# Last half of a DiT block: w_down and the second MLP product accumulated token by token in PSUM

## The chip, the cores and the metric

The kernel runs on one core of one Trainium2 chip. The core has TensorE (PE in the profile: matmuls, with the loads of the stationary operand as PEld), VectorE (DVE), ScalarE (ACT), GpSimd (POOL) and SyncE (SP, which issues nearly all DMAs). Matmuls write into PSUM, eight banks of 128 partitions x 512 fp32; DVE and ACT read the sums from there. The metric is the device time of one launch in microseconds (us), lower is better; for a kernel the median of several runs is given.

## The reference

A diffusion backbone of two layers on 256 latent tokens and 256 context tokens, 1024 features, all in fp32. Layer 0 mixes tokens with a convolution module, layer 1 with a bidirectional mLSTM of 4 heads of 512. After each mixer and each MLP stands a LayerNorm. In the last layer only the latent tokens are needed behind the mixer. The part that the change is about is the end of layer 1:

```python
def sq_relu_mlp(u, w1, w2):
    return jnp.square(jax.nn.relu(u @ w1)) @ w2
...
    y = (hn.astype(xc.dtype) + skip * xc) * jax.nn.silu(z)
    return y @ w_down                                  # (256 x 2048) @ (2048 x 1024)
...
        h = layer_norm(ALPHA * h + g1 * y, ln1_g[i], ln1_b[i])
        h = layer_norm(ALPHA * h + g2 * sq_relu_mlp(modulate(h, sh2, sc2), mlp_w1[i], mlp_w2[i]), ln2_g[i], ln2_b[i])
```

w1 is 1024 x 4096, w2 is 4096 x 1024. g1, g2, sh2 and sc2 are vectors over the 1024 features, made from the condition.

## The kernel before

**Products.** Each fp32 operand is split in two fp32r parts, hi and lo, and a product is hi·hi + hi·lo + lo·hi: three matmuls into one PSUM bank. `mm3` (L176 to L181) keeps a 128x128 block of the weight stationary and streams activations, so its result has features on the partitions and tokens along the row. `mm3t` (L183 to L187) keeps the activations of 128 tokens stationary and streams 512 columns of the weight, so its result has tokens on the partitions. Matmuls of the latent tokens alone stream 256 columns under `mm3`, and 512 under `mm3t`.

**Weights.** `raw_load` (L148) has SP fetch 1 MB at a time into one of three staging buffers `raw`. `split_w` cuts it in two pieces of 128x1024; ACT casts each to `wh` (L154), DVE subtracts to get `wl` (L155). There are four `wh` and four `wl` buffers (NW), handed out in turn; a staging buffer is free again after the lo split of its second piece. Other tiles come from pools in the same way: a piece of code that gets a buffer waits for the last reader of what it held.

**Order.** The code is written in the order of the computation, with some steps mixed by hand; a scheduler then fixes the order on each engine and puts in the semaphores. On each engine instructions run strictly in that order, so an instruction that waits holds up all behind it.

**The end of layer 1.** `Z.att` (L46) is the list of main and side steps of the attention part, run by the loop at L1378: `oN` is the o gate of head N, `G` `W` `A` are decay, weights and attend, `DN` is w_down of head N. A side step is advanced a number of times for each step of the main one. D0 runs beside o2, D1 and D2 beside A3, D3 by itself.

`down(h)` (L1354) takes the head's 512 rows of w_down and makes, for each of 8 blocks m of 128 features, 4 x 3 matmuls of 256 columns. A DVE instruction (L1366) then adds gate times the sum to the residual `hl[m]`, which lies feature by feature; this happens for each head. For the last head `hl[m]` also goes to `Norm.feed` (L417), which builds sums for the LayerNorm on DVE and ACT.

`ln.finish` (L446) sums over the partitions with small PE matmuls (L441), takes the root on ACT (L455), builds a diagonal (L462) and spreads the result over the rows with a matmul by ones (L467). `ln.apply` (L473, L474) normalises each block, and L1405 to L1407 make the MLP's input `u2`, hi on ACT and lo on DVE.

`mlp` (L823) runs in four chunks of 1024 hidden features: w1 for 8 blocks m (three matmuls of 256 columns for each of 8 kt), squared ReLU and split, then w2 for 8 blocks of output features, whose sums DVE adds to the residual (L854) after each chunk. A second Norm, the affine part on ACT (L1421) and eight transfers of 128 KB (L1422) of a features x tokens result end the kernel; the host transposes it. Creating a Norm puts a small Sqrt activation (`warm`, L403) into ACT's stream, which the scheduler has at the program's start.

## Time and profile before

| | us |
|---|---|
| median of 3 runs | 1737.08 (1736.88 to 1744.12) |
| the profiled execution | 1738.46 |
| its span in the profile | 1736.7 |
| PE busy | 1691.6 (97%) |
| DVE busy | 1071.7 (62%) |
| ACT busy | 736.3 (42%) |

The span is the stretch that the profile shows, from the first to the last recorded work; the rest of the time lies around it. In a timeline each row has the start, the duration, engine, line of the kernel, operation, output and input by name, and in brackets how long the engine stood idle before it and what ended that. Matmuls are pipelined: their durations overlap, and what one costs is read from the distance of the starts. "mm", "ln", "fl" and "cv" are names of PSUM banks (3, 2, 1 and 2 of them), the others are tiles in SBUF.

### The profile page before, as it was taken

The numbers are of one execution on the slowest core, as the hardware profiler recorded it, in microseconds if no ns is written. First come the engines' busy times: TensorE is split into PE (matmuls) and PEld (weight loads), VectorE is DVE, ScalarE is ACT, GpSimd is POOL, SyncE is SP. The second block draws the span as 40 slices with busy tenths as digits, with TensorE's granted clock in tenths as the row PEclk, the third lists the DMA queues.
The fourth block names the chain that finished last, engine by engine and source line by source line (L and its number), as shares of the span: only waits on it lengthen the run. The fifth ranks groups of instructions, "written<-read, shape, count | busy, mean of one in ns | idle before, by whom it ended". The sixth has DMA issues, their size and how long they took to land.

```text
span 1736.7 us, 25617 instructions
## 1 busy us (share of the span) xinstructions
PE 1691.6 (97%) x10282; PEld 1443.4 (83%) x10282; DVE 1071.7 (62%) x1975; ACT 736.3 (42%) x1159; POOL 31.8 (2%) x84
## 2 busy tenths in 40 slices
PE   8999999999999999999999999999999999989996
PEld 5655798888888999976787999998777888979996
DVE  5556897976665886762222543443687766886666
ACT  3411763232324465542333433432576645444443
POOL 0000000000000000000000000000021000000000
PEclk9999999999999999999999999999999999989998
DMA  9333534665554065577743622443545555535551
GB/s 359 128 118 122 215 126 146 218 218 194 194 194 170 28 220 170 160 237 253 264 146 126 223 99 96 150 157 132 183 158 188 186 206 204 184 112 180 189 176 49
DMA packets 60182, 298.61 MB, mean 172 GB/s; under 512 B 5986, under 2 KB 21858, under 8 KB 26656
## 3 DMA queue, kind: packets, MB, share of 16 engines
q1 hardware_dynamic: 42400, 282.29, 46.6%
q10 hardware_dynamic: 17664, 14.69, 2.5%
q8 instruction: 81, 1.33, 0.3%
q14 instruction: 37, 0.30, 0.1%
HBM read 281.22 MB, written 15.73 MB: 171 GB/s over the span
## 4 chain that ended last, share of the span: by engine, by line
PE 92%; DVE 3%; ACT 2%; DMA 1%; issue 1%; POOL 0%; SPq 0%; POOLq 0%; ACTq 0%
PE mm L177 23%; PE mm L181 23%; PE mm L180 23%; PE mm L187 3%; PE mm L185 3%; PE mm L186 3%; PE fl L297 1%; PE fl L647 1%; PE cv L716 1%; DVE wl L155 1%; PE ln L177 1%; PE ln L180 1%; PE ln L181 1%; DMA raw<-ada_w 1%; PE cv L185 1%
## 5 line engine op out<-in xcount | busy, mean ns | idle before, releaser
L155 DVE TENSOR_TENSOR wl<-raw,wh 128x1024 fp32r<-128x1024 f32 x354 | 432.4, 1225 | 357.7 <-ACT wh L154 356.9
L154 ACT CAST wh<-raw 128x1024 fp32r<-128x1024 f32 x354 | 368.2, 1048 | 615.0 <-PE mm L180 432.8
L180 PE MATMUL mm<-u,wh 128*128 128x256 f32 (+1 forms) x1400 | 447.2, 320 | 0.0
L177 PE MATMUL mm<-u,wh 128*128 128x256 f32 (+1 forms) x1272 | 397.7, 314 | 6.6 <-DVE E L673 2.0
L181 PE MATMUL mm<-u,wl 128*128 128x256 f32 (+1 forms) x1272 | 396.8, 313 | 1.1 <-DVE wl L155 1.1
L180 PEld LDWEIGHTS mm<-u,wh 128*128 128x128 f32 x1400 | 268.2, 192 | 18.4 <-DVE mv L482 0.8
L177 PEld LDWEIGHTS mm<-u,wh 128*128 128x128 f32 x1272 | 243.2, 192 | 30.5 <-issue 5.6
L181 PEld LDWEIGHTS mm<-u,wl 128*128 128x128 f32 x1272 | 244.3, 192 | 16.3 <-DVE wl L155 2.3
L177 PE MATMUL mm<-hid,wh 128*128 128x256 f32 (+1 forms) x512 | 165.9, 324 | 0.0
L180 PE MATMUL mm<-hid,wh 128*128 128x256 f32 (+1 forms) x512 | 165.3, 323 | 0.0
L181 PE MATMUL mm<-hid,wl 128*128 128x256 f32 (+1 forms) x512 | 165.3, 323 | 0.0
L177 PEld LDWEIGHTS mm<-hid,wh 128*128 128x128 f32 x512 | 97.4, 190 | 7.9 <-issue 0.2
L180 PEld LDWEIGHTS mm<-hid,wh 128*128 128x128 f32 x512 | 97.4, 190 | 7.7 <-issue 0.2
L181 PEld LDWEIGHTS mm<-hid,wl 128*128 128x128 f32 x512 | 97.4, 190 | 7.6
L177 PE MATMUL mm<-xm,wh 128*128 128x512 f32 x256 | 102.9, 402 | 0.0
L185 PE MATMUL mm<-wh,xl 128*128 128x512 f32 x256 | 101.0, 396 | 0.7 <-ACT wh L154 0.6
L186 PE MATMUL mm<-wh,xl 128*128 128x512 f32 x256 | 100.6, 393 | 0.6 <-DVE xl L155 0.6
L181 PE MATMUL mm<-xm,wl 128*128 128x512 f32 x256 | 100.3, 392 | 0.0
L187 PE MATMUL mm<-wl,xl 128*128 128x512 f32 x256 | 100.1, 394 | 0.2
L177 PE MATMUL mm<-qq,wh 128*128 128x272 f32 x256 | 73.9, 289 | 0.0
L180 PE MATMUL mm<-qq,wh 128*128 128x272 f32 x256 | 73.9, 289 | 0.0
L181 PE MATMUL mm<-qq,wl 128*128 128x272 f32 x256 | 73.8, 288 | 0.0
(411 smaller groups left out, 2745.7 us busy)
## 6 DMA issues: line engine op xcount, KB each, us to landing
raw<-w SPq DMA_DIRECT2D x64, 1024.0 KB, 4.9
raw<-ada_w SPq DMA_DIRECT2D x48, 1024.0 KB, 5.3
raw<-wo SPq DMA_DIRECT2D x32, 1024.0 KB, 4.9
raw<-wv SPq DMA_DIRECT2D x16, 1024.0 KB, 6.5
raw<-wqT SPq DMA_DIRECT2D x16, 1024.0 KB, 5.1
raw<-wq SPq DMA_DIRECT2D x16, 1024.0 KB, 4.9
raw<-wk SPq DMA_DIRECT2D x16, 1024.0 KB, 4.9
raw<-pw SPq DMA_DIRECT2D x10, 1024.0 KB, 6.2
```

The costliest lines, as they stand in the source:

```text
L154: c = nc.scalar.copy(hi, src)
L155: nc.vector.tensor_tensor(lo, src, hi.bitcast(F32), op=ALU.subtract)
L177: a = nc.tensor.matmul(ps, wh, xh, start=start, stop=False)
L180: nc.tensor.matmul(ps, wh, xl, start=False, stop=False)
L181: nc.tensor.matmul(ps, wl, xh, start=False, stop=stop)
L185: nc.tensor.matmul(ps, xh, wh, start=start, stop=False)
L186: nc.tensor.matmul(ps, xl, wh, start=False, stop=False)
L187: nc.tensor.matmul(ps, xh, wl, start=False, stop=stop)
L297: a = nc.tensor.matmul(ps[32 * j:32 * j + 32], cs[:, kt, 14 - 2 * v:46 - 2 * v], blocks[kt], start=first and kt < 4, stop=last and kt >= 4 ...
L647: nc.tensor.matmul(wqs[0][32 * j:32 * j + 32, :], wgp[0][:, kt, :], raw[:, j * 512:(j + 1) * 512], start=kt == 0, stop=kt == ET - 1, tile_ ...
L716: return nc.tensor.matmul(o[r:r + 64, :], g_[:, r:r + 64], ps_[b][i], start=i == 0, stop=i == 1, tile_position=(0, r))
```

## The change

Four things change, all in layer 1.

1. **Token-major residual.** `hl` becomes four tiles `hl[t][h_]`: 128 tokens (t) by 512 features (h_). In up_z a new side step `rows()` fills them: 8 DVE instructions, 16 PE transposes and 4 copies on ACT.
2. **w_down.** `down(h)` uses `mm3t`: activations stationary, weights streamed 512 wide, the sum of all heads in four PSUM banks `dacc` (three "mm" and the "fl"), 192 matmuls of 512 in place of 384 of 256. The host lays `wdown` out anew. D0 leaves the side of o2 and stands with D1 and D2, beside A3. The last head has its weights split in pieces of 512 and its matmuls grouped by (t, h_); after each group DVE multiplies by the gate's row, adds to `hl` and takes bn_stats. The gate's rows come from a small DRAM tile (written by ACT's queue during layer 0) broadcast to 128 partitions. The LayerNorm becomes a row-wise one: aggregate, Sqrt, reciprocal and a subtract-and-multiply on DVE, then 16 transposes back to features, from which `affine_half` makes `u2`, with hi and lo side by side in one tile of 512 columns.
3. **MLP.** For a block of w1 one matmul streams hi and lo together (512 columns, stationary `wh`) and one streams hi alone (256 columns, stationary `wl`); ACT copies the lo half of the sum, DVE adds it and squares. The w2 product is an `mm3t` with the hidden activations stationary, summed over all 32 blocks in four banks (two "ln", two "cv"). Two blocks of w1 and two of w2 alternate. The last four w2 blocks are grouped by (t, h_).
4. **Tail.** Five rows of 1024 (gain and bias of both LayerNorms, the gate) are broadcast to 128 partitions; DVE finishes the LayerNorm row-wise, and four transfers of 256 KB write the output token by token.

```diff
-    att = [['o0', 'G0 W0 W1', 2], ['o1', 'A0 W2', 1.6], ['o2', 'A1 W3 D0', 2.1], ['o3', 'A2', 1], ['D1 D2', 'A3', 1.2], ['D3', '', 0]]
+    att = [['o0', 'G0 W0 W1', 2], ['o1', 'A0 W2', 1.6], ['o2', 'A1 W3', 1.6], ['o3', 'A2', 1], ['D0 D1 D2', 'A3', 1.2]]
...
+    g_dr = [dp.tile([D], F32, name=f"g_dr{i}") for i in range(2)]
+    for i, o in enumerate((2 * DT, 5 * DT)):
+        nc.scalar.dma_start(g_dr[i].rearrange("(f p) -> p f", p=P), ada[1][:, o:o + DT, 1])
...
-                for kt in range(4):
-                    mm3(ps, *kcol(w, (i % 2) * 4 + kt), *yy[h][kt], kt == 0, kt == 3)
-                nc.vector.scalar_tensor_tensor(hl[m], ps, g1[:, m:m + 1], hl[m], op0=ALU.mult, op1=ALU.add)
...
+        if last:
+            for t in range(2):
+                for h_ in range(2):
+                    for kt in range(4):
+                        down_mm(h, kt, t, h_, ws[kt])
+                    tm, r = tmp("E"), hl[t][h_]
+                    nc.vector.tensor_tensor(tm, dacc[t, h_], g1r[h_], op=ALU.mult)
+                    nc.vector.tensor_tensor(r, r, tm, op=ALU.add)
+                    nc.vector.bn_stats(st1[:, t, h_, :], r)
+                    yield
+
+    def down_mm(h, kt, t, h_, w):
+        yh, yl = yy[h][kt]
+        mm3t(dacc[t, h_], yh[:, BLK[t]], yl[:, BLK[t]], w[0][h_], w[1][h_], h == 0 and kt == 0, h == H - 1 and kt == 3)
...
+        root(mv1[:, t], st1[:, t])
+        for h_ in range(2):
+            nc.vector.tensor_scalar(hl[t][h_], hl[t][h_], mv1[:, t, 0:1], mv1[:, t, 2:3], op0=ALU.subtract, op1=ALU.mult)
+            for j in range(4):
+                f = 4 * h_ + j
+                nc.tensor.transpose(trs[f // 2][:, f % 2 * C + t * P:f % 2 * C + (t + 1) * P],
+                                    hl[t][h_][:, j * P:(j + 1) * P], ident)
...
+        affine_half(t[:, LO], t[:, HI], trs[f // 2][:, f % 2 * C:f % 2 * C + C], 1, ca, cb, f)
...
+    for r, src in zip(rws, [rows_d[i] for i in range(4)] + [g_dr[1]]):
+        nc.sync.dma_start(r, row(src))
...
+        a = lambda stop: nc.tensor.matmul(ps, wh, u2[kt], start=kt == 0, stop=stop)
+        b = lambda: nc.tensor.matmul(ps[:, LO], wl, u2[kt][:, LO], start=False, stop=False)
...
+        mm3t(facc[t, h_], hid[j][:, t * P:(t + 1) * P], hid[j][:, C + t * P:C + (t + 1) * P], w[0][:, sl], w[1][:, sl],
+             j == 0, j == NF - 1)
...
+    for m in range(4, NF, 2):
+        up(m)
+        up(m + 1)
+        dn(m - 4)
+        dn(m - 3)
+        if m == 6:
+            for t in range(2):
+                for h_ in range(2):
+                    r, sl = hl[t][h_], slice(h_ * T, (h_ + 1) * T)
+                    nc.vector.scalar_tensor_tensor(r, r, ALPHA, ln1g[:, sl], op0=ALU.mult, op1=ALU.mult)
+                    nc.vector.scalar_tensor_tensor(r, ln1b[:, sl], ALPHA, r, op0=ALU.mult, op1=ALU.add)
...
+            nc.vector.tensor_tensor(tm, facc[t, h_], g2r[:, sl], op=ALU.mult)
+            nc.vector.tensor_tensor(r, r, tm, op=ALU.add)
+            nc.vector.bn_stats(st1[:, t, h_, :], r)
+        root(mv1[:, t], st1[:, t])
...
-    ln.finish()
-    for f in range(DT):
-        xn = ln.apply(f)
-        t = tmp("E")[:, :C]
-        nc.scalar.activation(t, xn, AF.Identity, scale=V("ln2_g1", f), bias=V("ln2_b1", f))
-        nc.sync.dma_start(out[f * P:(f + 1) * P, :], t)
```

The scheduler's order shows where steps now stand. The line numbers in rows of the changed kernel are its own.

First SP's queue at the end of w_down, before. `raw` is a staging buffer, `wdown` w_down, `zs_dr` the stored z gate of a head, and `w_1` stands for both weights of the second MLP:

```order
L150 DMA raw_13164<-v_dr_5290 128x2048
L150 DMA raw_13250<-wdown 128x2048
L150 DMA raw_13330<-zs_dr_5294 128x2048
L150 DMA raw_13351<-wdown 128x2048
L150 DMA raw_13441<-wdown 128x2048
L150 DMA raw_13507<-wdown 128x2048
L150 DMA raw_13578<-wdown 128x2048
L150 DMA raw_13686<-w_1 128x2048
L150 DMA raw_13696<-w_1 128x2048
```

And in the changed kernel, up to the broadcasts of the five rows:

```order
L150 DMA raw_13321<-wdown 128x2048
L150 DMA raw_13355<-w_1 128x2048
L150 DMA raw_13365<-w_1 128x2048
L150 DMA raw_13375<-wdown 128x2048
L150 DMA raw_13393<-wdown 128x2048
L150 DMA raw_13664<-w_1 128x2048
L150 DMA raw_13722<-w_1 128x2048
L150 DMA raw_13756<-w_1 128x2048
L1464 DMA row_13554<-rows_d 128x1024
L1464 DMA row_13555<-rows_d 128x1024
L1464 DMA row_13558<-g_dr_5302 128x1024
L150 DMA raw_13814<-w_1 128x2048
```

The first two loads of w1 now stand ahead of the last head's two loads of w_down, and the five rows stand between loads of the MLP's weights.

Second, DVE behind the LayerNorm of w_down's result, before (`lc` are the small statistics, `S` and `u` make the lo part of the MLP's input):

```order
L458 SCALAR_TENSOR_TENSOR lc_13721<-lc_13709,lc_13721 128x2
L462 TENSOR_TENSOR L_13724<-ident,lc_13721 128x512
L473 TENSOR_TENSOR hl_5901<-hl_5901,ln_13726 128x256
L474 TENSOR_TENSOR hl_5901<-hl_5901,ln_13726 128x256
L473 TENSOR_TENSOR hl_5901<-hl_5901,ln_13726 128x256
L1406 TENSOR_SCALAR S_13743<-hl_5901,ca_13729,cb_13730 128x256
```

And in the changed kernel (`mv` are mean and deviation, `row` the broadcast rows; L497 writes the lo part):

```order
L1411 BN_AGGR mv_11256<-st_11255 128x2
L1413 RECIPROCAL mv_11256<-mv_11256 128x1
L1445 TENSOR_SCALAR hl_5307<-hl_5307,mv_11256 128x512
L1445 TENSOR_SCALAR hl_5308<-hl_5308,mv_11256 128x512
L1537 SCALAR_TENSOR_TENSOR hl_5305<-hl_5305,row_13554 128x512
L1537 SCALAR_TENSOR_TENSOR hl_5306<-hl_5306,row_13554 128x512
L497 TENSOR_TENSOR u_13514<-S_13515,u_13514 128x256
L497 TENSOR_TENSOR u_13519<-S_13520,u_13519 128x256
L1538 SCALAR_TENSOR_TENSOR hl_5305<-row_13555,hl_5305 128x512
L497 TENSOR_TENSOR u_13524<-S_13525,u_13524 128x256
```

The scaling of the residual by the gain's row (L1537), which the code writes inside the MLP's loop, stands ahead of the lo parts of the MLP's input.

Third, PE in the MLP of the changed kernel, the end of one block of w1 and the start of a block of w2 (`hid` are the hidden activations):

```order
L1470 MATMUL mm_14810<-u_13544,wh_14806 128x512
L1471 MATMUL mm_14810<-u_13544,wl_14807 128x256
L1471 MATMUL mm_14810<-u_13549,wl_14807 128x256
L1470 MATMUL mm_14810<-u_13549,wh_14806 128x512
L185 MATMUL ln_13660<-wh_14836,hid_14619 128x512
L186 MATMUL ln_13660<-wh_14836,hid_14619 128x512
L187 MATMUL ln_13660<-wl_14837,hid_14619 128x512
L185 MATMUL ln_13661<-wh_14836,hid_14619 128x512
```

Before, all rows of the MLP are of the form of this one, in threes by L177, L180 and L181:

```order
L177 MATMUL mm_14480<-u_13756,wh_14518 128x256
L180 MATMUL mm_14480<-u_13756,wh_14518 128x256
L181 MATMUL mm_14480<-u_13756,wl_14519 128x256
L177 MATMUL mm_14480<-u_13763,wh_14518 128x256
L180 MATMUL mm_14480<-u_13763,wh_14518 128x256
```

Two matmuls of 512 and 256 columns take the place of three of 256 in the first product; in the second the sums stay in the four banks from one block to the next.

More of the change, by code (lines that the diff above doesn't have):

```diff
@@ L1371, in chain, with row, root @@
+    def row(src):
+        return src.rearrange("(o c) -> o c", o=1).broadcast_to([P, src.shape[0]])
+    def root(mv, st):
+        nc.vector.bn_aggr(mv[:, 0:2], st.rearrange("p h c -> p (h c)"))
+        nc.scalar.activation(mv[:, 2:3], mv[:, 1:2], AF.Sqrt, bias=eps)
+        nc.vector.reciprocal(mv[:, 2:3], mv[:, 2:3])
+    g1r = []
     def chain(names):
         for n_ in names.split():
-            if n_[0] == "D":
-                yield from down(int(n_[1]), "mm" if main_is_down else "fl")
-            else:
-                yield from dict(G=decay, W=weights, o=gate_o, A=attend)[n_[0]](int(n_[1]))
+            yield from dict(G=decay, W=weights, o=gate_o, A=attend, D=down)[n_[0]](int(n_[1]))
@@ L1395, in hybrid_kernel @@
+    for _ in last:
+        pass
     close_pool()
     ca, cb = comb(1, "ln1_g1", "ln1_b1", "sc2", "sh2", (1,))
[L1398 removed]
     qf = open_pool("qf")
[L1400 removed]
+    U, HD = maker(qf, "u", DT), maker(qf, "hid", 8)
     u2 = []
     for f in range(DT):
[L1403 to L1408 removed]
```

178 lines of the change are left out of this document (127 added, 51 removed).

## The prediction

> **What bounds the kernel now.** I read the page first: the engines' shares and the chain that ended last.
>
> ```profile
> PE 1691.6 (97%) x10282; PEld 1443.4 (83%) x10282; DVE 1071.7 (62%) x1975; ACT 736.3 (42%) x1159; POOL 31.8 (2%) x84
> ...
> PE 92%; DVE 3%; ACT 2%; DMA 1%; issue 1%; POOL 0%; SPq 0%; POOLq 0%; ACTq 0%
> ```
>
> TensorE (PE) carries 92% of the chain. The time falls only by what leaves PE's stream, or by what fills a gap in it. The busy time by stretch says where gaps are:
>
> ```profile
> 1500.00:1550.00 50.00, 39.07 (x284) 0.86 0.35 116
> 1531.00:1535.00 4.00, 3.60 (x17) 0.50 0.01 2
> 1550.00:1700.00 150.00, 150.00 (x1252) 1.00 0.55 188
> 1700.00:1737.00 37.00, 23.00 (x174) 0.81 0.08 29
> ```
>
> Columns: stretch, its length, PE busy (count), granted clock, DMA share, GB/s. Only two stretches of the changed part have idle PE: the LayerNorm ahead of the second MLP, and the tail. Between them the MLP is solid: 1252 matmuls of 256 columns in 150 us, 0.1198 us each. The timeline of PE shows what a matmul of 512 costs in the gate_o stage, and what a set of four transposes does to that spacing:
>
> ```profile
> 1439.83 0.39 PE L187 MATMUL mm<-wl,xl 128*128 128x512 f32 x1
> ...
> 1449.81 0.39 PE L186 MATMUL mm<-wh,xl 128*128 128x512 f32 x1
> ...
> 1457.17 0.60 PE L1338 MATMUL ln<-ident,og 128*128 128x128 f32 x4
> 1457.52 0.48 PE L185 MATMUL mm<-wh,xl 128*128 128x512 f32 x1
> 1457.83 0.40 PE L186 MATMUL mm<-wh,xl 128*128 128x512 f32 x1
> ```
>
> The first two rows are the ends of an unbroken run of 45, so starts lie 9.98 / 44 = 0.2268 us apart. Two of 256 take 0.2396, one of 512 takes 0.2268: each pair merged saves 0.013 us. Four transposes take about 0.43 (from 1457.17 to 1457.83, less one matmul).
>
> **The matmul stream.** w_down falls from 384 matmuls of 256 to 192 of 512. The MLP falls from 1536 of 256 to 256 pairs of (512 + 256) and 384 of 512. The columns streamed are the same; 192 + 640 = 832 instructions go.
> - D0 to D2, the first three heads of w_down: 288 × 0.1198 = 34.5; now 144 × 0.2268 = 32.6. **-1.9**.
> - MLP: the stretch from its first matmul (1531.40) to its last (1719.49 + 0.12, below) is 188.2. Of that 1536 × 0.1198 = 184.0; about 1.8 is the slow clock at its start, the rest Norm's matmuls and small stalls. Now 256 × (0.2268 + 0.1198) = 88.7 and 384 × 0.2268 = 87.1, together 175.8; 1.9 for the same slow start and 0.5 for stalls: 178.2. **-10.0**. For other engines I charge nothing. Four weight blocks (two of w1, two of w2) give PE 2 × 2.77 + 2 × 2.72 = 11.0 us; DVE has four lo splits of 1.23 in them and six instructions of 256 columns, which cost at most the 0.74 of a split of 512 (both rows below): 9.3 us, still covered. If that cover were gone, PE would wait for DVE's excess in each of 16 such rounds.
> - The gate rows: two small transfers on ACT's queue in the layer before, two broadcasts on SP's queue ahead of D0, five at the MLP's start. An issue takes SP 0.33 (rows below), and SP's queue is not in the chain (SPq 0%): nothing, apart from the waits below.
> - Up_z gains 16 transposes to make the residual token-major: 4 × 0.43. **+1.7** (between 0, if they fill idle PE, and 2.4, if each costs as the pair in the row with its 0.60).
>
> **w_down's last head and the LayerNorm.** Before, from the trace:
>
> ```profile
> 1517.11 0.28 PE L181 MATMUL mm<-og,wl 128*128 128x256 f32 x1
> 1521.42 0.72 PE L441 MATMUL ln<-inv_c,x 128*128 128x1 f32 x4 [4.03 <-DVE x L407]
> ...
> 1527.67 2.04 PE L467 MATMUL ln<-L,ones 128*128 128x512 f32 x2 [2.06 <-DVE L L462]
> 1531.40 1.01 PE L177 MATMUL mm<-u,wh 128*128 128x256 f32 x3 [1.68 <-ACT u L1405]
> ...
> 1534.13 0.41 PE L177 MATMUL mm<-u,wh 128*128 128x256 f32 x1
> 1534.34 0.41 PE L180 MATMUL mm<-u,wh 128*128 128x256 f32 x1
> ...
> 1535.40 0.28 PE L177 MATMUL mm<-u,wh 128*128 128x256 f32 x1
> ```
>
> D3's 96 matmuls of 256 take 11.5, so D2 ended about 1505.7, and from there to the MLP's first matmul it is 25.7 us. After the gap matmuls start 0.213 apart until 1535.40: the granted clock is low for 4 us (the stretch 1531 to 1535 above).
>
> The same distance in the new kernel is put together from these rows (DVE's first five, then ACT's):
>
> ```profile
> L155 DVE TENSOR_TENSOR wl<-raw,wh 128x1024 fp32r<-128x1024 f32 x154 | 188.5, 1227 | 72.8 <-ACT wh L154 72.2
> ...
> L1296 DVE TENSOR_TENSOR og<-mm,bo 128x512 f32<-128x512 f32 x16 | 10.8, 682 | 0.9 <-PE mm L187 0.9
> L155 DVE TENSOR_TENSOR og<-og,og 128x512 fp32r<-128x512 f32 x8 | 5.9, 740 | 0.2 <-ACT og L154 0.2
> L1320 DVE BATCH_NORM_STATS2 gst<-og 128x6 f32<-128x512 f32 x8 | 5.5, 689 | 0.1
> L1319 DVE TENSOR_TENSOR og<-og,og 128x512 f32<-128x512 f32 x8 | 5.5, 688 | 0.1
> ```
>
> ```profile
> L154 ACT CAST wh<-raw 128x1024 fp32r<-128x1024 f32 x154 | 159.4, 1047 | 165.7 <-PE mm L180 79.5 <-PE mm L186 54.5 <-PE cv L186 6.6
> ...
> L154 ACT CAST og<-og 128x512 fp32r<-128x512 f32 x8 | 4.9, 618 | 3.9 <-DVE og L1344 3.9
> ...
> L1325 ACT ACTIVATE gmv<-gmv,eps 128x2 f32<-128x2 f32 x4 | 1.2, 299 | 0.7 <-DVE gmv L1321 0.6
> ```
>
> Landing times, of a w_down load of 1 MB and of the o bias, which is a row of 4 KB broadcast to 128 partitions (512 KB):
>
> ```profile
> L150 SPq DMA_DIRECT2D raw<-wdown x8: 327/328/328, 1378.8 to 1496.3; - x8
> ...
> DMA to landing us min/median/max: 4.8/4.9/6.4
> ```
>
> ```profile
> L1279 SPq DMA_DIRECT2D bo<-bo_d x4: 328/328/333, 1233.6 to 1417.9; - x4
> ...
> DMA to landing us min/median/max: 4.1/5.5/6.4
> ```
>
> The new order on SP puts two loads of w1 ahead of D3's two loads, and the first of D3's waits for a staging buffer that is freed by the lo split (1.23) of the second w1 block. That split follows its cast (1.05), which needs a weight slot that D2's second quarter (of four, one for each 128 rows of the weight) frees. With that quarter's end as 0, the load is issued at 1.05 + 1.23 + 0.33 + hand-overs = about 2.85. D2's last two quarters give PE 24 × 0.2268 and four transposes (A3's), so D2 ends at 5.95. The load lands at 2.85 + 4.9 = 7.75, the first cast of 512 takes 0.6: D3 starts near 8.3 and **PE idles 2.3** where before it idled nothing (bounds: 1.6 from the shortest hand-overs, 4.4 with the longest landing 6.4). Behind this wait stand D3 and all that follows; DVE's eight lo splits of 512 (0.74) set the pace of D3's first token block, done at 8.3 + 5.9, about 14; the third group of twelve matmuls ends at 16.7. Nine matmuls into the last group, at 18.7, PE comes to eight transposes that wait about 1 for DVE L1445; with them and the last three matmuls the group ends near 21.3. Then DVE does L1398, L1399, L1400, aggregate, root and two L1445 (0.68 + 0.69 + 0.69, some 0.2 for the small aggregate, 0.30 for the root on ACT and 0.2 for its reciprocal, 2 × 0.6): 25.4 with hand-overs.
>
> Now a wait that did not exist. The LayerNorm's row of gains is sent by SP only after L1398 of the last group has run (22.0), and lands 4.1 to 6.4 later, near 27.8. DVE's L1537, which reads it and is only needed at the end of the kernel, stands ahead of the first lo split L497 of the MLP's input. Behind it wait L497 and so the MLP. First MLP matmul: 27.8 + two L1537 hidden in part + L497 = **28.6**, which is 22.7 after D2's end, against 25.7. **-3.0**, range 20 to 26: -5.7 to +0.3. Cast and copy on ACT are hidden behind the same row.
>
> **Tail.** Before:
>
> ```profile
> 1719.49 0.28 PE L181 MATMUL mm<-hid,wl 128*128 128x256 f32 x1
> ...
> 1725.05 2.05 PE L467 MATMUL ln<-L,ones 128*128 128x512 f32 x2 [1.99 <-DVE L L462]
> ```
>
> ```profile
> 1733.60 0.60 ACT L1421 ACTIVATE E<-hl,vecs 128x256 f32<-128x256 f32 x1 [0.19 <-DVE hl L474]
> ```
>
> From the last matmul's end to the span's end, 1736.7, it is 17.1; the last 2.5 are the last transfer and the end. Now after the last matmul: L1545, two L1546, two L1547, aggregate, two L1551, two L1552. Ten instructions at 0.60 spacing (a row of 0.69 overlaps the next by about 0.09) are 5.9, then 0.3 hand-over and 2.5 for a transfer twice as large: 8.7. **-8.4** (-7 to -9.5: DVE at its full durations of 0.69 and 0.75, or at a spacing below 0.55).
>
> **Start.** Two activations that load the Sqrt table fall away, and with them two table loads:
>
> ```profile
> 4.13 1.28 ACT L403 ACT_TABLE_LOAD   x1
> ...
> 45.50 1.28 ACT L669 ACT_TABLE_LOAD   x1
> ```
>
> ```profile
> 52.08 0.47 PE L177 MATMUL mm<-u,wh 128*128 128x512 f32 x1 [2.05 <-DVE E L673]
> ```
>
> The second load stands ahead of the first epilogue, and PE waits 2.05 for that epilogue's product. **-1.0** (0 if the weights' DMA covers it, -2.5 if both count).
>
> Sum: -1.9 - 10.0 + 1.7 - 3.0 - 8.4 - 1.0 = -22.6. The profiled run took 1738.5, its span 1736.7 with 1.8 around it; that is 1.4 above the median 1737.1. From the run: 1715.9; from the median: 1714.5. **Predicted: 1715.**
>
> [...]
>
> **Rivals.**
> - *Waits bite less* (1709): D3's loads land at the first moment (-2.3), the row lands in 4.1 (-1.4), start and tail at their better ends (-2). For: a load alone on an idle bus. Against: four other transfers queue with it. 0.15.
> - *Waits bite more* (1723): landing 6.4 (+2.1), D3 run at the halved clock after its wait (+2.0), row at 6.4 (+0.9), two stalls of 1.4 at the transposes of A3 and D3. For: the halved clock after the old gap; but that gap was 14 us, this one 2.3. 0.13.
> - *No saving per instruction* (1726): a 512 matmul beside 256 ones, each with another weight load, is spaced 0.24, so 11.1 of the sum stay. For: the weight loads (PEld) are busy 83% of the span. Against: the 0.2268 rows come with weight loads too. 0.03. [...]
> - *Slower* (1738): the five row broadcasts. They stand ahead of the second w2 load on SP's queue, and the second row's L1538 stands ahead of the third L497. If a row takes r us of the queue, that w2 block is split at about 22.3 + 5r + 6.5, and PE needs it near 56: it decides from r = 5.4, and costs 5 for each us beyond; at r = 10 it costs 23, and the gain is gone. For: nothing shows five in a row. Against: a single one is landed in 4.1 to 6.4 with its latency included, so r is likely 2. 0.04.
> - *The change moves something I do not see*, up to +18 in sum, ending within 0.5%: 0.03.
>
> Likeliest: 0.62. 0.5% of 1737 is 8.7 us, about what a measurement of this kernel can tell from no change, so faster means below 1728.4: the forecast and the first three rivals, less 0.03 for their upper ends, 0.90; within 0.5% 0.06; slower 0.04. The range starts below the first rival, 1705, and ends past the second and third, 1727.
>
> **What would show it.** A pair of 512 and 256 spaced 0.3466 in the MLP, first MLP matmul to last 177 to 180 us; an idle of 1.6 to 4.4 on PE just before D3, put down to ACT's cast; DVE L1537 waiting for a DMA about 5 us, PE idle 6 to 8 behind it; 8 to 9.5 us after the last matmul. An MLP longer than 184, or PE waiting for casts of w2's third block, would make it wrong.

## The result

The changed kernel takes **1727.56 us** (median of 6 runs, 1725.27 to 1729.37) against 1736.98 before (1736.42 to 1744.12); the ratio is 0.9937, 95% interval 0.9919 to 0.9954. It is faster, by 9.4 us and not by the 22 forecast, and 0.6 us above the forecast's range. Run once more later, it took 1724.21 (4 runs, 1721.71 to 1728.23; ratio 0.9929, 0.9910 to 0.9949). Single times that stood 6 to 10 us above the rest came with a lower mean granted clock (1720.92 at 0.989 in run 9, where 1711.25 had 0.996), and in the kernel before too (1744.06 at 0.985, where 1736.89 had 0.990). The profiled execution took 1725.27, the least of the six, with a span of 1723.6; so 2.3 us by which the median is higher are not in the stretches below.

The changed kernel's page, the engines and the chain of what ended last:

```profile
PE 1681.7 (98%) x9450; PEld 1400.1 (81%) x9450; DVE 1052.4 (61%) x1887; ACT 730.0 (42%) x1148; POOL 33.6 (2%) x84
...
PE 91%; DVE 4%; ACT 2%; DMA 1%; issue 1%; POOL 0%; SPq 0%; DVEq 0%; ACTq 0%; POOLq 0%
```

PE is busy 10 us less, and the span is 13 us shorter. To see where, both timelines of PE are cut at the same five matmuls: A, the one behind a short wait near 180 us, where layer 0's products start; B, the one in up_z that waits for DVE's first epilogue there; C, the o gate's at 1235.90 (before) that waits 0.62 for a lo split; F, the first of the last MLP; G, the end of its last (its start and the distance to the next, 0.12 or 0.23). "Forecast" is the prediction's term for the stretch.

| stretch | before | changed | difference | forecast |
|---|---|---|---|---|
| start to A | 180.75 | 179.08 | -1.7 | -1.0 |
| A to B: layer 0 | 433.14 | 438.31 | **+5.2** | 0 |
| B to C: up_z, up_x, v, q, k | 622.01 | 625.26 | **+3.3** | +1.7 |
| C to F: o gate, w_down, LayerNorm | 295.50 | 290.76 | -4.7 | -4.9 |
| F to G: MLP | 188.21 | 180.42 | -7.8 | -10.0 |
| G to the end | 17.13 | 9.73 | -7.4 | -8.4 |
| sum | 1736.7 | 1723.6 | -13.2 | -22.6 |

So the w_down part, the MLP and the tail paid 19.9 us where 23.3 were forecast; 8.5 us are lost in layer 0 and up_z, where 1.7 were forecast, hundreds of microseconds ahead of any matmul that the change makes cheaper. ACT in layer 0's MLP, in the changed kernel, and the same cast in the one before:

```profile
523.00 0.43 ACTq L945 DMA_DIRECT2D g_dr<-ada  x1
...
541.13 1.14 ACT L154 CAST u<-raw 128x512 fp32r<-128x512 f32 x2 [6.14 <-DMA raw<-w]
```

```profile
536.61 1.14 ACT L154 CAST u<-raw 128x512 fp32r<-128x512 f32 x2 [0.20 <-DMA raw<-w]
```

The second gate row's transfer goes out at 523.00 on ACT's queue. The weight load that SP issues behind it, at 530.35, lands 10.76 us later (the loads of this stretch in the kernel before took 4.9 to 7.3, as far as their landing is recorded), and ACT stands 6.14 us for it. The DMA view of 525 to 545, of the changed kernel and then of the one before:

```profile
DMA packets 1369, 2.31 MB, mean 116 GB/s; under 512 B 1088, under 2 KB 1088, under 8 KB 1088
...
q10 hardware_dynamic: 1040, 0.00, 2.9%
```

```profile
DMA packets 491, 3.62 MB, mean 181 GB/s; under 512 B 49, under 2 KB 49, under 8 KB 49
```

1040 packets of almost no bytes (q10 is ACT's queue) stand among 327 of weights. They themselves take only 2.9% of the engines' time, 9 ns each, and are through by 529.3. What grows long behind them are packets of the next weight load: in the trace's list of packets, 27 of 8 KB that start between 531 and 537 take 2.0 to 6.9 us each, where the mean in the kernel before was 0.3 to 0.4. The same stands in all seven profiled executions with these pieces (the changed kernel and runs 1, 3, 4, 5, 6 and 11: 21 to 29 weight packets over 2 us in this stretch) and in none of the six without (the kernel before and runs 2 and 7 to 10: 0). Why the pieces do this the traces do not show. The stretches of the changed kernel and of the one before (length, PE busy, granted clock, DMA share, GB/s):

```profile
530.00:541.00 11.00, 11.00 (x51) 1.00 0.80 97
556.00:561.00 5.00, 5.00 (x29) 0.66 0.86 349
615.13:618.54 3.41, 1.15 (x9) 1.00 0.09 30
618.54:621.95 3.41, 3.41 (x18) 0.50 0.26 85
```

```profile
530.00:541.00 11.00, 11.00 (x50) 1.00 0.28 95
```

From 530 to 541 about the same GB/s (95 before, 97 now) take 0.28 of the DMA engines before and 0.80 now. PE uses up its lead and then waits 2.15, and the granted clock falls behind the wait (1.00 from 530 to 541, 0.66 from 556 to 561); a fall behind a wait comes again in up_z (1.00, then 0.50), where the wait is 2.46 and for another thing. The row of the kernel before stands last:

```profile
555.99 0.39 PE L177 MATMUL mm<-hid,wh 128*128 128x256 f32 x1 [2.15 <-ACT hid L154]
```

```profile
617.39 0.39 PE L177 MATMUL mm<-u,wh 128*128 128x256 f32 x1 [2.46 <-DVE E L940]
...
619.00 0.41 PE L181 MATMUL mm<-u,wl 128*128 128x256 f32 x1
619.21 0.41 PE L177 MATMUL mm<-u,wh 128*128 128x256 f32 x1
```

```profile
613.89 0.39 PE L177 MATMUL mm<-u,wh 128*128 128x256 f32 x1 [1.60 <-DVE E L940]
```

In up_z starts lie 0.21 apart where the granted clock was 0.50 (618.54 to 621.95) and 0.12 apart where it was 1.00; behind each of the two waits the low clock lasts 3.4 us and costs 1.6 (16 matmuls, each 0.09 to 0.10 more). Before, the wait at B was 1.60 and the clock stayed at 1.00.

The places that the prediction spoke of, in the changed kernel: the last head and the LayerNorm on PE, then DVE:

```profile
1508.62 0.39 PE L187 MATMUL fl<-wl,x 128*128 128x512 f32 x1
1512.78 0.78 PE L185 MATMUL mm<-xl,og 128*128 128x512 f32 x1 [3.77 <-ACT xl L154]
1513.36 0.63 PE L186 MATMUL mm<-xl,og 128*128 128x512 f32 x1
1513.78 0.63 PE L187 MATMUL mm<-xl,og 128*128 128x512 f32 x1
...
1530.42 1.12 PE L1448 MATMUL ln<-ident,hl 128*128 128x128 f32 x4 [3.59 <-DVE hl L1445]
...
1533.41 0.79 PE L1470 MATMUL mm<-u,wh 128*128 128x512 f32 x1 [1.02 <-DVE u L497]
```

```profile
1504.57 0.69 DVE L155 TENSOR_TENSOR og<-og,og 128x512 fp32r<-128x512 f32 x1
1505.18 0.87 DVE L1359 SCALAR_TENSOR_TENSOR og<-ln,vecs,raw 128x256 f32<-128x256 f32 x2
1505.96 1.22 DVE L155 TENSOR_TENSOR wl<-raw,wh 128x1024 fp32r<-128x1024 f32 x1
...
1531.72 1.29 DVE L1537 SCALAR_TENSOR_TENSOR hl<-hl,row 128x512 f32<-128x512 f32 x2 [0.90 <-DMA row<-rows_d]
1532.94 0.75 DVE L497 TENSOR_TENSOR u<-S,u 128x256 fp32r<-128x256 f32 x2
```

PE waits 3.77 for the last head's weights and starts it at the low clock (0.50 from 1512.84 to 1516.25; 0.42 to 0.58 from one 512 start to the next). The wait for the row, on the other hand, is 0.90. In the MLP, first the spacing in the four blocks of w1 prepared ahead of it, then the only stall, then the first product at steady state:

```profile
1537.46 0.39 PE L1470 MATMUL fl<-u,wh 128*128 128x512 f32 x1
...
1541.62 0.39 PE L1470 MATMUL fl<-u,wh 128*128 128x512 f32 x1
...
1546.66 0.50 PE L1470 MATMUL mm<-u,wh 128*128 128x512 f32 x1 [0.37 <-ACT wh L154]
1547.92 0.39 PE L1471 MATMUL mm<-u,wl 128*128 128x256 f32 x1 [0.76 <-DVE wl L155]
...
1639.92 0.40 PE L1470 MATMUL mm<-u,wh 128*128 128x512 f32 x1
1640.16 0.28 PE L1471 MATMUL mm<-u,wl 128*128 128x256 f32 x1
...
1641.34 0.40 PE L1470 MATMUL mm<-u,wh 128*128 128x512 f32 x1
```

Twelve pairs of 512 and 256 lie between the starts of the first two rows, 4.16 us or 0.347 a pair. At steady state four pairs take 1.42; over the twelve whole rounds between 1558 and 1687, 16 pairs take 5.63 us, 0.352 a pair. And the tail, on DVE:

```profile
1712.40 1.41 DVE L1552 SCALAR_TENSOR_TENSOR E<-hl,mv,row 128x512 f32<-128x512 f32 x2
1713.73 1.28 DVE L1545 TENSOR_TENSOR E<-cv,row 128x512 f32<-128x512 f32 x2
```

### The profile page after: what moved, and what is told of

It is laid out like the page before. It is cut to its first block, busy times and chain, and to the rows that moved or that the text cites. A ratio compares the mean times of both kernels' runs of the same rounds, so it can differ in the third digit from the quotient of the medians.

```text
span 1723.6 us, 23808 instructions
## 1 busy us (share of the span) xinstructions
PE 1681.7 (98%) x9450; PEld 1400.1 (81%) x9450; DVE 1052.4 (61%) x1887; ACT 730.0 (42%) x1148; POOL 33.6 (2%) x84
## 4 chain that ended last, share of the span: by engine, by line
PE 91%; DVE 4%; ACT 2%; DMA 1%; issue 1%; POOL 0%; SPq 0%; DVEq 0%; ACTq 0%; POOLq 0%
PE mm L177 19%; PE mm L181 19%; PE mm L180 19%; PE mm L1470 3%; PE mm L185 3%; PE mm L187 3%; PE mm L186 3%; PE mm L1471 2%; PE cv L185 1%; PE cv L187 1%; PE cv L186 1%; PE fl L297 1%; DVE wl L155 1%; PE fl L647 1%; PE cv L716 1%; PE ln L177 1%
## 5 line engine op out<-in xcount | busy, mean ns | idle before, releaser
L155 DVE TENSOR_TENSOR wl<-raw,wh 128x1024 fp32r<-128x1024 f32 x350 | 427.0, 1223 | 357.0 <-ACT wh L154 354.4
L180 PE MATMUL mm<-u,wh 128*128 128x256 f32 (+1 forms) x1152 | 376.9, 327 | 0.0
L177 PE MATMUL mm<-u,wh 128*128 128x256 f32 (+1 forms) x1024 | 328.2, 321 | 5.8 <-DVE E L673 2.9
L181 PE MATMUL mm<-u,wl 128*128 128x256 f32 (+1 forms) x1024 | 327.0, 320 | 0.0
L180 PEld LDWEIGHTS mm<-u,wh 128*128 128x128 f32 x1152 | 220.6, 192 | 18.1 <-DVE mv L482 0.8
L177 PEld LDWEIGHTS mm<-u,wh 128*128 128x128 f32 x1024 | 196.2, 192 | 27.6 <-issue 8.9
L181 PEld LDWEIGHTS mm<-u,wl 128*128 128x128 f32 x1024 | 196.4, 192 | 15.9 <-DVE wl L155 1.7
L177 PE MATMUL mm<-xm,wh 128*128 128x512 f32 x256 | 102.8, 402 | 0.0
L181 PE MATMUL mm<-xm,wl 128*128 128x512 f32 x256 | 100.3, 392 | 0.0
L177 PE MATMUL mm<-hid,wh 128*128 128x512 f32 (+1 forms) x256 | 94.0, 367 | 2.2 <-ACT hid L154 2.2
L180 PE MATMUL mm<-hid,wh 128*128 128x512 f32 (+1 forms) x256 | 93.8, 367 | 0.1
L181 PE MATMUL mm<-hid,wl 128*128 128x512 f32 (+1 forms) x256 | 93.6, 366 | 0.0
L1470 PE MATMUL mm<-u,wh 128*128 128x512 f32 x248 | 89.2, 402 | 1.4 <-DVE u L497 1.0
L357 DVE CUSTOM_DVE_ANT_0 raw<-raw,cb,vecs 128x1024 f32<-128x1024 f32 x48 | 61.1, 1281 | 33.9 <-DMA raw<-ada_w 33.6
L180 PE MATMUL mm<-qq,wh 128*128 128x272 f32 x256 | 73.9, 289 | 0.0
L177 PE MATMUL mm<-qq,wh 128*128 128x272 f32 x256 | 73.9, 289 | 0.0
L181 PE MATMUL mm<-qq,wl 128*128 128x272 f32 x256 | 73.8, 288 | 0.0
L177 PEld LDWEIGHTS mm<-xm,wh 128*128 128x128 f32 x256 | 48.1, 188 | 22.5 <-issue 6.7
```

What stands on the lines that cost most here:

```text
L155: nc.vector.tensor_tensor(lo, src, hi.bitcast(F32), op=ALU.subtract)
L177: a = nc.tensor.matmul(ps, wh, xh, start=start, stop=False)
L180: nc.tensor.matmul(ps, wh, xl, start=False, stop=False)
L181: nc.tensor.matmul(ps, wl, xh, start=False, stop=stop)
L357: nc.vector.tensor_tensor_reduce(dump, w, cb[:, s, :], 1.0, vecs[:, o:o + 1], ALU.mult, ALU.add, accum_out=ada[1][:, m, s:s + 1])
L1470: a = lambda stop: nc.tensor.matmul(ps, wh, u2[kt], start=kt == 0, stop=stop)
```

## The experiments

All ratios are against the kernel before, in the same session on the same chip. The stretches are those of the table above, from each run's one profiled execution. The changed kernel's own medians differ by 3.4 us (1727.56 and 1724.21), and the times of runs 3 to 6 lie 2 to 6 us below those that their theory 1 gave; what these runs show is therefore read from the stretches, not from the times.

| run | median us | ratio (95%) | A | A to B | B to C | C to F | F to G |
|---|---|---|---|---|---|---|---|
| 1 before, with the gate transfers | 1740.60 | 1.0017 (1.0006 to 1.0028) | 179.67 | 435.06 | 622.09 | 295.26 | 188.88 |
| 2 gate row by PE | 1724.10 | 0.9938 (0.9914 to 0.9962) | 179.19 | 433.78 | 627.07 | 290.45 | 180.40 |
| 3 last head's loads first | 1721.02 | 0.9904 (0.9875 to 0.9932) | 179.69 | 438.92 | 625.22 | 287.46 | 180.31 |
| 4 hi and lo apart | 1725.98 | 0.9938 (0.9913 to 0.9962) | 177.69 | 435.95 | 625.29 | 289.87 | 184.60 |
| 5 scaling held back | 1724.38 | 0.9912 (0.9882 to 0.9942) | 178.98 | 435.37 | 625.27 | 291.26 | 181.48 |
| 6 table loads put back | 1722.31 | 0.9901 (0.9874 to 0.9928) | 178.61 | 436.82 | 623.53 | 290.44 | 180.47 |
| 7 edits 2, 3 and 5 together | 1721.49 | 0.9895 (0.9865 to 0.9925) | 179.45 | 433.80 | 627.29 | 285.81 | 180.93 |
| 8 and the residual's steps first | 1715.01 | 0.9859 (0.9834 to 0.9883) | 179.65 | 433.77 | 623.78 | 286.02 | 180.80 |
| 9 and the table loaded early | 1712.25 | 0.9865 (0.9840 to 0.9891) | 177.49 | 432.41 | 623.85 | 285.78 | 180.04 |
| 10 and two splits later | 1712.77 | 0.9857 (0.9842 to 0.9871) | 178.75 | 432.41 | 623.86 | 285.74 | 179.85 |
| 11 the changed kernel again | 1724.21 | 0.9929 (0.9910 to 0.9949) | 177.29 | 435.98 | 625.27 | 291.56 | 181.09 |

**Run 1: the kernel before, and nothing but the two small transfers.** Put ahead of up_z's code, unread:

```diff
+    g_dr = [dp.tile([D], F32, name=f"g_dr{i}") for i in range(2)]
+    for i, o in enumerate((2 * DT, 5 * DT)):
+        nc.scalar.dma_start(g_dr[i].rearrange("(f p) -> p f", p=P), ada[1][:, o:o + DT, 1])
```

> The kernel before, with nothing added but the two transfers that write the gate rows (1024 pieces of 4 bytes each) on ACT's queue at the place where the changed kernel issues them; nothing reads what they write. Theory 1 (the pieces hold the 16 DMA engines, so a weight load of layer 0's MLP lands late): ACT waits some 6 us for that load near 535 to 540, PE idles about 2 us and runs at the low clock for 3 us behind it, and the time rises by 3 to 5 us, to 1740 to 1742. Theory 2 (the layer 0 loss of the changed kernel comes from the moved residual steps and the new order): no change, 1737 within 1.

Measured: 1740.60, 3 to 4 us slower (0.17%, 0.06 to 0.28). ACT, then PE:

```profile
540.86 1.14 ACT L154 CAST u<-raw 128x512 fp32r<-128x512 f32 x2 [5.55 <-DMA raw<-w]
```

```profile
555.65 0.39 PE L177 MATMUL mm<-hid,wh 128*128 128x256 f32 x1 [1.90 <-ACT hid L154]
```

The same wait for the same load stands in a kernel in which nothing else was touched (issued at 530.67, it lands 10.17 later), so theory 1 holds but for the clock: in this execution PE's wait was 1.90, the clock did not fall, and layer 0 lost 1.9. That is half of what the medians differ by; the profiled execution of the kernel before is itself 1.4 above its median.

**Run 2: the gate row without small pieces.** The gate vector (128x8) is transposed on PE, and written as 8 rows of 512 bytes:

```diff
-        nc.scalar.dma_start(g_dr[i].rearrange("(f p) -> p f", p=P), ada[1][:, o:o + DT, 1])
+        tr = psum("ln")
+        nc.tensor.transpose(tr[:DT, :P], ada[1][:, o:o + DT, 1], ident)
+        nc.scalar.copy(gt[:, i, :], tr[:DT, :P])
+        nc.scalar.dma_start(g_dr[i].rearrange("(f p) -> f p", p=P), gt[:, i, :])
```

> The changed kernel, but each gate vector is transposed on PE (128x8 to 8x128), copied, and written by 8 rows of 512 bytes in place of 1024 pieces of 4 bytes. Theory 1: the wait for the weight load in layer 0 is gone, layer 0 ends 3.5 to 5 us earlier (the first matmul of up_z behind its wait near 613 in place of 617.4), the time is 1722 to 1724. Theory 2: layer 0 takes as long as in the changed kernel, 1727 to 1728.

Layer 0 takes 433.78, 4.5 less than in the changed kernel, with B at 612.97. But B to C is 1.8 longer: the order in up_z shifted, and PE meets two waits there in place of one:

```profile
612.97 0.39 PE L177 MATMUL mm<-u,wh 128*128 128x256 f32 x1 [2.04 <-DVE E L940]
```

```profile
618.17 0.39 PE L181 MATMUL mm<-u,wl 128*128 128x256 f32 x1 [1.60 <-DVE wl L155]
```

Theory 1 holds for layer 0; of the 4.5 us, 2.7 arrived at C, and the ratio, 0.9938, is the changed kernel's. One thing was not kept apart: with the edit the transfers also go out later, at 609.92 and 610.79, behind layer 0's weight loads. So the run shows that layer 0 loses next to nothing without the pieces (433.8 against 433.1 before the change); it does not show that 8 rows of 512 bytes at 523 would have cost nothing.

**Run 3: the last head's loads ahead of w1's.** `down` of the last head loads and splits its weights, then yields, and the w1 loads follow:

```diff
-    pre1 = []
-    for g_ in range(2):
-        rx = raw_load(w1_1[g_, 0])
-        for m in range(2):
-            pre1.append(split_w(rx[:, m * 1024:(m + 1) * 1024]))
     last = down(H - 1)
+    next(last)
+    pre1 = []
+    for g_ in range(2):
+        rx = raw_load(w1_1[g_, 0])
+        for m in range(2):
+            pre1.append(split_w(rx[:, m * 1024:(m + 1) * 1024]))
```

> The changed kernel with the last head's two loads of w_down and their splits put ahead of the two loads of w1. Theory 1 (the 3.8 us idle and the low clock at the last head come from the loads' order): the idle ahead of the last head is under 0.5 us, its matmuls start at full clock; of the 5.4 us some 2 come back, because the row's transfer now ends later than all else ahead of the MLP (the scaling by the row stands ahead of the last block's normalisation). From the end of the third head to the MLP's first matmul 20 to 22 in place of 24.5, time 1723 to 1725. Rival (the loads are hidden anyway, DVE's splits set the pace): no change, 24 to 25 us and 1727 to 1728.

```profile
1510.33 0.39 PE L187 MATMUL fl<-wl,x 128*128 128x512 f32 x1
1510.56 0.39 PE L185 MATMUL mm<-xl,og 128*128 128x512 f32 x1
...
1524.82 1.09 PE L1450 MATMUL ln<-ident,hl 128*128 128x128 f32 x4 [3.22 <-DVE hl L1447]
...
1528.95 1.12 PE L1450 MATMUL ln<-ident,hl 128*128 128x128 f32 x4 [2.19 <-DVE hl L1447]
```

The idle ahead of the last head is gone, its first matmul follows 0.23 after the third head's last, at full clock. From that last matmul's end to the MLP's first it is 20.7 (1510.56 to 1531.29) in place of 24.6; C to F is 3.3 less, although this execution has a stall of 0.78 in the o gate that the changed kernel's does not have. Some of the 5.4 us came back, not at the row as was expected but at the transposes: PE waits 3.22 + 2.19 there in place of 3.59, where DVE now has w1's splits.

**Run 4: hi and lo in two matmuls of 256.**

```diff
-        a = lambda stop: nc.tensor.matmul(ps, wh, u2[kt], start=kt == 0, stop=stop)
+        def a(stop):
+            nc.tensor.matmul(ps[:, LO], wh, u2[kt][:, LO], start=kt == 0, stop=False)
+            nc.tensor.matmul(ps[:, HI], wh, u2[kt][:, HI], start=False, stop=stop)
```

> The changed kernel, but in the first MLP product the matmul of 512 columns (hi and lo side by side) is two of 256 again: 256 instructions more, the same columns. Theory 1 (12.8 ns for each instruction): the MLP is 3.3 us longer, 183.7 in place of 180.4 from its first matmul to its last, 1730 to 1731. [...]

By the time alone an instruction has no price (1725.98, inside the changed kernel's own spread), the stretch says otherwise. F to G is 184.6. Some of that is a start 1.7 earlier, since the first three matmuls need only the hi halves; from 1530.48, where the stream runs on, it is 182.9 against 180.4, so 2.5 more. At steady state a round's 16 triples of 256 take 5.75 (48 instructions) and 16 pairs of the changed kernel 5.63 (32): 7.5 ns for an instruction, against the 12.8 of the prediction's rows (0.2396 for two of 256, less 0.2268 for one of 512). The rows of a triple:

```profile
1601.84 0.28 PE L1471 MATMUL mm<-u,wh 128*128 128x256 f32 x1
1601.96 0.28 PE L1472 MATMUL mm<-u,wh 128*128 128x256 f32 x1
...
1602.20 0.28 PE L1471 MATMUL mm<-u,wh 128*128 128x256 f32 x1
```

A triple is 0.36, as before the change; a pair is 0.352 in the rounds and not 0.347. In the four prepared blocks, whose pairs go to four banks in turn, a pair is 0.347 and a triple 0.36, which makes 13 ns for an instruction, as forecast. So an instruction had a price in these two executions, 13 ns where the banks take turns and 7.5 in the rounds, where one bank takes eight pairs in a row; whether the banks are the reason was not tried. In this execution layer 0 took 435.95, 2.4 less than in the changed kernel's profile, and A came 1.4 earlier, which is why the total hides it.

**Run 5: the scaling by the rows kept in its place.**

```diff
-                    nc.vector.scalar_tensor_tensor(r, r, ALPHA, ln1g[:, sl], op0=ALU.mult, op1=ALU.mult)
+                    tc.keep_in_program_order(
+                        nc.vector.scalar_tensor_tensor(r, r, ALPHA, ln1g[:, sl], op0=ALU.mult, op1=ALU.mult))
```

> The changed kernel, but the scaling of the residual by the broadcast rows is held in its written place inside the MLP, so that it no longer stands ahead of the lo parts of the MLP's input on DVE. Theory 1 (read from the trace of the changed kernel: the row lands 0.9 us after DVE is ready, and most of that is covered by ACT): the MLP's first matmul comes 0.7 to 1 us earlier after the last head, 1726 to 1727. Rival (the prediction's step: DVE waits about 5 us for the row): 3 to 5 us earlier, 1723 to 1725.

C to F is 291.26, with a stall of 0.77 in the o gate that the changed kernel's profile does not have; without it 290.5, against 290.76. The time, 1724.38, would fit the rival, but the stretch does not: the wait of 5 us that the prediction put on the row is not there to be gained, and even the 0.7 of theory 1 is not. By itself the edit gives 0.3.

**Run 6: the table loads put back.**

```diff
+    for _ in range(2):
+        nc.scalar.activation(con.tile([P, 1], F32, name=nm("warm")), eps, AF.Sqrt)
```

> The changed kernel with the two small Sqrt activations put back, which the scheduler places at the program's start with a table load of 1.28 us each time the table changes. Theory 1 (the changed kernel's earlier start is the missing table loads): the first matmul near 179.1 comes near 180.7 again, 1.6 us later, and the time is 1728.5 to 1729.5. Rival (the earlier start comes from something else, or a DMA sets that stage): 179.1 as before, 1727 to 1728.

A came at 178.61, not at 180.7, though the load stands again where it stood:

```profile
4.13 1.28 ACT L1455 ACT_TABLE_LOAD   x1
```

```profile
48.00 0.50 PE L177 MATMUL mm<-u,wh 128*128 128x512 f32 x1 [0.58 <-ACT wh L154]
...
50.82 0.47 PE L177 MATMUL mm<-u,wh 128*128 128x512 f32 x1 [2.08 <-DVE E L673]
```

With the loads PE waits 0.58 + 2.08 near 50 us, without them 2.87 at once; the sums are near each other, and the matmul behind the wait starts at 50.8 to 52.1 in the three executions with the loads (the kernel before, runs 1 and 6) and at 51.1 to 52.3 in the ten without. So theory 1 finds no support. A lies anywhere from 177.3 to 179.7 in the executions without the loads, a wider range than the 1.6 us in question: below 178 in the three in which the clock stayed up between 50 and 66 us, above it in the seven in which it fell there (in the changed kernel to 0.50 from 51.93 to 55.35 and from 62.17 to 65.59). The time, 1722.31, is below what either theory gave. This run is also the one whose clock stayed up behind the wait of 2.46 at B:

```profile
611.24:614.65 3.41, 1.73 (x12) 1.00 0.02 5
614.65:618.06 3.41, 2.63 (x22) 1.00 0.33 115
618.06:621.47 3.41, 3.41 (x31) 1.00 0.11 38
```

and B to C is 623.53, 1.7 less than in the five executions in which it fell behind this wait.

**Runs 7 and 8: the edits together.** Run 7 has the edits of 2, 3 and 5. Run 8 has besides:

```diff
-        next(side if i < DT else side2, None)
-    for s_ in (side, side2):
+        next(side2 if i < 4 else side, None)
+    for s_ in (side2, side):
```

> The changed kernel with three edits together: gate rows by PE transposes, the last head's loads first, the scaling by the rows held back. If the losses found so far are separate and add up (3.5, 3.8 to 6.6 and 0.8 us): 1716 to 1720. If one gain only uncovers the next wait (DVE ahead of the MLP, or up_z): 1721 to 1723.

> As the run before, and in up_z the residual's 8 DVE steps, 16 transposes and copies are put ahead of the other side work (the first layer's normalisation of the context tokens) rather than behind it. Theory 1 (the wait of 1.6 us for a lo split in up_z comes from that side work standing ahead of it on DVE): 1.5 to 2 us less than that run, 1714 to 1718. Rival (up_z then waits for the same work later): the same time within 1 us.

Run 7: layer 0 keeps its 4.5 and C to F falls by 5.0, more than run 3's 3.3, or 4.1 without run 3's stall of 0.78 in the o gate. So about 0.9 remain for the scaling by the rows once the loads are early, where run 5 alone had 0.3. But up_z is as long as in run 2 (627.29), and the single times go from 1718.5 to 1724.3; by the median it is the second case of what was expected. Run 8 takes 3.5 from up_z, as its wait of 1.6 for a lo split is gone and the clock stays up behind the wait of 2.04 at B: 1715.01, with 4 runs from 1714.66 to 1715.69.

**Runs 9 and 10: two further steps.** Run 9 loads the Sigmoid table behind the last root of layer 0. Run 10 also moves two of w1's splits behind the first token block's statistics:

```diff
+    nc.scalar.activation(con.tile([P, 1], F32, name=nm("warm")), lns[0].ms[:, 0:1], AF.Sigmoid)
...
+        if t == 0:
+            pre(1)
```

> As the run with the four edits (1715.0), and one Sigmoid activation that depends on the last root of layer 0's LayerNorm, so that ACT loads the Sigmoid table while it waits and not ahead of up_z's first epilogue. Theory 1 (the table load of 1.28 us is the end of PE's wait of 2.04 there): the wait falls to about 0.8, the time to 1713.5 to 1714.5. Rival (the wait ends with DVE's normalisation steps, not with ACT): 1715 within 0.7.

> As the run before, and two of the four w1 splits ahead of the MLP are written behind the first token block's statistics. Theory 1 (PE's wait of 3.2 us at the last head's transposes is DVE busy with 4.7 us of w1 splits): the wait falls by 1 to 2.4 us and the MLP starts that much earlier, 1711.5 to 1713. Rival (DVE's whole work up to the MLP is the bound, the order within it changes nothing): the same time as the run before within 0.7.

Run 9: PE's wait at B is

```profile
609.90 0.39 PE L177 MATMUL mm<-u,wh 128*128 128x256 f32 x1 [0.65 <-DVE E L941]
```

0.65 in place of 2.04, and A to B is 1.36 shorter, as theory 1 has it. The time is 1712.25, but one of its four runs took 1720.92, and its ratio (0.9865) is not apart from run 8's. Run 10: the first wait at the transposes falls, the second grows by as much. In run 9 and then in run 10:

```profile
1514.07 0.63 PE L1456 MATMUL ln<-ident,hl 128*128 128x128 f32 x4 [3.22 <-DVE hl L1453]
...
1517.12 1.11 PE L1456 MATMUL ln<-ident,hl 128*128 128x128 f32 x4 [1.74 <-DVE hl L1453]
```

```profile
1514.23 0.63 PE L1460 MATMUL ln<-ident,hl 128*128 128x128 f32 x4 [2.03 <-DVE hl L1457]
...
1518.35 1.11 PE L1460 MATMUL ln<-ident,hl 128*128 128x128 f32 x4 [3.05 <-DVE hl L1457]
```

C to F is 285.74 against 285.78. The rival holds: DVE's whole work up to the MLP is the bound there, not its order.

**Run 11: the changed kernel again.**

> The changed kernel once more, beside the two runs above on the same chip. Theory 1 (the 4-byte pieces meet the weight load at another moment in each execution, so the loss in layer 0 varies from 1.5 to 5 us): the single times spread over 3 us or more, 1724 to 1729, while the two kernels without those pieces stay within 1.5 us. Rival (the spread is that of the chip): all three spread alike.

Its four times spread over 6.5 us (1721.71 to 1728.23), run 10's over 2.8 and run 9's over 2.3 but for one that stands 7.7 above the rest. So the two kernels without the pieces do not stay within 1.5 us, and theory 1 is not shown. In its profiled execution layer 0 took 435.98 and not 438.31. Over the seven executions with the small pieces layer 0 takes 435.1 to 438.9, in the five variants without them 433.8 (three) or 432.4 (two): the loss does vary. PE's wait there is 1.37 to 2.15, and in the two executions of 438.3 and 438.9 the low clock follows it, in the other five not. How much of the spread of the times comes from this is open, as one execution of each run is profiled.

## Why the prediction was wrong

The direction was right and so was the mechanism of each saving; the size was not. One term was set to nothing, one cost was too small and three savings were too large.

- **The gate rows: "nothing".** This is the step that failed. I priced the two transfers by SP's issue time of 0.33 and by SP's share of the chain; they are not on SP's queue, and their cost is not the issue. The row that would have told was in the change itself: 1024 elements of 4 bytes each. What they hold up is the weight load issued behind them, which landed 9.6 to 11.5 us after its issue in the seven executions with them, and for which ACT had 0.20 to wait even before the change. Run 1 shows it with nothing else changed (+1.9 us), and the executions without the pieces (runs 2 and 7 to 10) have none of it. Of the +5.2 in the table the wait of PE is 2.15, the low clock behind it 1.6, and 0.86 is the longer wait at B, which ends this stretch; the last 0.6 was not traced.
- **Up_z: +1.7, measured +3.3.** Where the clock stayed up, B to C is 1.5 (run 6) to 1.8 (run 8) longer than before, which fits what was said of the transposes. The rest is the low clock behind the wait at B, which grew from 1.60 to 2.46. I had looked for work added and not for waits that a new order makes. Why this wait grew no run shows. In both kernels it ends with the first epilogue, whose step on ACT stands behind a cast and a table load of 1.28; PE ran dry 1.88 after that cast began in the kernel before and 0.80 after in the changed one. Run 9, which moves the table load, cut such a wait from 2.04 to 0.65.
- **The last head and LayerNorm: -3.0, measured -1.1** (24.6 against 25.7). The idle ahead of the last head was placed rightly and is 3.77, inside the bounds of 1.6 to 4.4 but far from 2.3. I had the lo split start right behind its cast; it stood behind A3's steps L155 and L1359 on DVE until 1505.96, though its cast was done at 1504.02. And the clock fell behind that idle, which I had put to a rival. The row wait was mis-sized the other way: SP sends the row behind the step I said, at 1527.63, it lands 4.0 later, and DVE is ready for L1537 only 0.9 before that; my working made this wait 2.4 (25.4 to 27.8), my list of signs about 5. From C to the end of D2 the gain is 3.6, where D0 to D2 were to give 1.9; where the other 1.7 comes from was not tried. That C to F comes out near its forecast is therefore luck.
- **MLP: -10.0, measured -7.8.** 178.2 was to be 180.4. The pair is spaced 0.352 and not 0.3466 (14 rounds, 224 pairs, 1.2 us), though in the four prepared blocks it is 0.347, and behind these blocks PE stalls for 0.37 + 0.76 at the first casts and splits.
- **Tail: -8.4, measured -7.4.** The ten instructions take the spacing that was said, but the two L1545 follow one another from 1713.73: the first could have started 2.5 us earlier, and DVE was still busy with the first token block's L1551 and L1552. The transfer took 2.0 to 2.1 to land.
- **Start: -1.0.** No such term shows in run 6. The 1.7 in the table is within what executions differ by.

Of the rivals, "waits bite more" (1723) named two of the mechanisms, the long idle and the low clock behind it, at the wrong price. The slow rival did not come true: the five broadcasts were issued within 2.6 us and no w2 block waited for its load. "No saving per instruction" is refuted by run 4, with 13 ns for an instruction in the prepared blocks and 7.5 in the MLP's rounds. The 11.1 us of that rival no run shows: 832 instructions at the 12.8 ns of the prediction's rows are 10.6 us.

The best version here keeps the change and adds four edits (run 8): 1715.01, ratio 0.9859 (0.9834 to 0.9883) to the kernel before. That this is the time that the prediction gave the change alone is a coincidence. Runs 9 and 10 are at 1712, not told apart from it by the intervals.

## What to carry to other kernels

Price every DMA that a change adds by its number of pieces and by the load that is in flight with it, not by its bytes or its issue: one transfer of 4 KB in 4-byte pieces cost more here (layer 0 was 1.9 us longer in run 1, which has two of them) than five broadcast rows of 512 KB (DVE waited 0.90 for the first of them, and for no other). When a change moves work between engines, compare the waits at the start of each stage before and after, also in stages that it does not speed up, and price a new wait of PE by the wait and by the low clock that may follow it (1.6 us behind each of two waits here). When a total moves less than the sum, cut both timelines at the same matmuls before looking for a cause: here the largest loss lay a thousand microseconds ahead of the edited stage, and a total (run 4) hid a stage's 2.5 us altogether.

## What the runs showed of the hardware

The granted clock fell after waits of PE much shorter than the 14 us ahead of the MLP in the kernel before (1517.39 to 1531.40): behind 2.15 in layer 0 in two of two executions (the changed kernel and run 3), behind 2.46 at B in five of six (the changed kernel and runs 3, 4, 5 and 11, and not run 6). In each of the thirteen profiled executions the trace's clock records change only on a grid of 3.41 us, kept from start to end, and the low stretch behind such a wait is one step of it: in the changed kernel 0.50 from 557.10 to 560.51 and from 618.54 to 621.95. It began 0.05 to 1.15 us after PE's restart (1.11 and 1.15 in these two cases). What went with a fall was the idle time of PE within one step: from 100 us on, a step at full clock with 2.14 us or more of it was followed by a low one in 39 of 39 cases of the thirteen executions, one with 1.0 to 1.76 in 2 of 47; in the kernel before and the changed one together it is 7 of 7 (2.14 to 3.41) and 0 of 5 (1.14 to 1.74). The two of 47 are runs 2 and 7, with 1.60 and 1.58; why they fell and others of 1.6 did not is open. The wait of 2.46 put 2.25 to 2.47 into one step where the clock fell, and 1.68 and 0.78 into two steps in run 6, where it did not. So the 1.6 us of low clock in up_z were paid in five of these six executions.

In the changed kernel a transfer of 1024 pieces of 4 bytes took 9 ns for each of them, but of the load issued behind it 27 packets of 8 KB took over 2 us (21 to 29 in the seven executions with the pieces), where the mean in the kernel before was 0.3 to 0.4, and it landed 10.76 us after its issue (9.6 to 11.5 in the seven). The DMA engines' share was 0.80 in place of 0.28 for 11 us (530 to 541) at 97 GB/s in place of 95.
